# One decoder layer on one NeuronCore: first modulation in groups of 2, 4, 4, 4 and 2 tiles, requested ahead, and six weight slots with extra ones later

## The chip, the cores and the metric

One core of a Trainium2 chip runs the whole program. TensorE (PE) multiplies, VectorE (DVE), ScalarE (ACT) and GpSimd (POOL) do the rest, and SyncE (SP) issues the large transfers from HBM. The metric is the device time of the core in microseconds (us).

## What is computed

One layer with `T = 256` tokens and `D = 2048` channels, all in float32. `c_act` is `silu(c)`; the six parts of the modulation are columns of one matrix-vector product.

```python
mod = (c_act @ w_ada[l] + b_ada[l])[:, None, :]
sh1, sc1, gt1, sh2, sc2, gt2 = jnp.split(mod, N_MOD, axis=-1)
h = rms_norm(x, g_mix_norm[l]) * (1.0 + sc1) + sh1
proj = h @ w_in[l]            # differential attention and gated linear attention (GLA) follow
mix = jnp.concatenate([od, og], axis=-1) @ w_o[l]
x = x + gt1 * mix
h2 = rms_norm(x, g_ffn_norm[l]) * (1.0 + sc2) + sh2
u, g = jnp.split(h2 @ w_up[l], 2, axis=-1)
act = jax.nn.gelu(causal_dwconv(g, w_conv[l], b_conv[l]), approximate=False) * u
x = x + gt2 * (act @ w_down[l])
return rms_norm(x, g_final)
```

## The kernel before

**Units.** All large weights come in units of 512 KB. A unit of `w_in`, `w_o`, `w_up` or `w_down` (two tiles of 128 rows by 512 columns) is loaded by `load_unit` (L107) into one of five `raw` slots, split by ACT into its rounded half `wh` (L110) and by DVE into the rest `wl` (L111), and used by 24 matmuls of 256 columns (`b_block`, L129) or 12 of 512 columns (`a_block`, L163): every product is the sum of three. A unit of `w_ada` goes into the same five slots (`raw_a`, L228 or L231); DVE multiplies it by the column of `c_act` and adds it to `acc` (L241, the first one by ACT, L239), and once all of a group are in, PE sums `acc` over its rows (`ps_mod`, L221), and three short DVE instructions (L253 to L256) make shift and scale. There are 192 units of `w_ada` and 392 of the others.

**Stages.** The first projection takes the 16 tiles of the normalised input `hT` in four rounds (`KGROUPS` 2, 4, 4, 6), here called g0 to g3, and in each round nine column blocks of `w_in` (9, 18, 18 and 27 units). Round g needs shift and scale of its own tiles, so `need` drains their part of the modulation. In before this part is cut into eight groups of two tiles (`ADA1`), each eight units of `w_ada` made of two DMAs of 256 KB. The remaining three blocks of `w_in` (24 units, `LATER`) and the output projection `w_o` (32 units, four column blocks) run beside GLA and attention. Then `rsqrt_m2` (L190 to L194) and `norm_T` (L272 to L282) make `h2T`, and the up projection begins with seven column chunks over tiles 0 to 3 and then over tiles 4 to 7 (56 units), whose sums wait in `spill` tiles; the rest of up (120 units) and down (88 units) follow.

**Order.** The units of `w_ada` are made by generators in the list `bg`, in the order first modulation (64 units), gate 1 (32), second modulation `ada2` (4 times 16), gate 2 (32). Each `load_unit` adds `rate` to a credit and lets one step of `bg` run for each whole one; `drain` runs a group to its end at once. The rates are 1.2 in g0 to g2, 1.0 in g3, 0.3 in `LATER` and `w_o`, 1.05 in the first 56 units of up, 0.25 after. The second modulation's first group is drained after `w_o`. From this program a scheduler makes the order on each engine, by a simulated timeline, unless an instruction is pinned by `keep_in_program_order`; the memory of a slot is given out in the program's order.

**Low rank and tables.** After the second block of every half round, two matmuls for each tile (`ps_low`, L687) add to the low-rank gate input `lowT`. `setup_consts`, run in g0, loads `wlow` (64-byte rows) and the attention tables on ACT's queue and makes the tables on POOL and DVE.

Of the kernel before, what the change touches and what calls it, by code (L numbers as in the profile page):

```python
# [15 lines left out]
P = 128  # L16
# [16 lines left out]
R_K, R_LAST, R_LATER, R_WO, R_SP, R_UP = 1.2, 1.0, 0.3, 0.3, 1.05, 0.25  # L33
# [4 lines left out]
ADA1 = (2, 2, 2, 2, 2, 2, 2, 2)  # L38
# [8 lines left out]
def tile_decoder_layer(  # L47
# [13 lines left out]
    RAW, WH, WL = 5, 3, 3  # L61
# [13 lines left out]
    fg, fcredit, frate = [], [0.0], [0.0]  # L75

# [19 lines left out]

    def load_unit(view, kt, c0):
# [8 lines left out]
        raw = stage.tile([P, 2, 512], F32, tag="raw", name="raw", bufs=RAW)  # L106
        nc.sync.dma_start(out=raw, in_=view[:, kt:kt + 2, c0:c0 + 512])  # L107
        h = stage.tile([P, 2, 512], F32R, tag="wh", name="wh", bufs=WH)
        l = stage.tile([P, 2, 512], F32R, tag="wl", name="wl", bufs=WL)
# [97 lines left out]
    def ada_gen(segs, width, c0, finish, psp, on_pe=(), by_rows=False):  # L207
# [6 lines left out]
        n_end = sum(k in on_pe for k in (KT - 2, KT - 1)) // 2 * 2  # L214
# [9 lines left out]
        for kt in range(0, KT, per):  # L224
            raw = stage.tile([P, per, n], F32, tag="raw", name="raw_a", bufs=RAW)
            rv = raw.rearrange("p k (s n) -> p k s n", n=width)
            if per == 1:
                nc.sync.dma_start(out=rv[:, 0], in_=w_ada4[:, kt, segs[0]:segs[-1] + 1, c0:c0 + width])  # L228
            else:
                for i, sg in enumerate(segs):  # L230
                    nc.sync.dma_start(  # L231
                        out=rv[:, :, i], in_=w_ada4[:, kt:kt + per, sg, c0:c0 + width])
            for j in range(per):
# [13 lines left out]
        finish(acc if by_rows else ps)  # L247
# [47 lines left out]
    colst = t1.tile([3 * KT, P], F32, tag="w4", name="colst", bufs=3)  # L295
    bst = t1.tile([6 * KT, P], F32, tag="w4", name="bst", bufs=3)
# [33 lines left out]

    def setup_consts():
        dlam = t1.tile([P, 6, 64], F32, tag="w4", name="dlam", bufs=3)
        dl2 = dlam[:, 4:6]
        wlow = t1.tile([P, KT, 16], F32, tag="w4", name="wlow", bufs=3)
        cz = t1.tile([P, NTB, T], F32, tag="w4", name="cz", bufs=3)
        nc.scalar.dma_start(out=wlow, in_=w_in_v[:, :, C_LOW:C_LOW + 16])
        nc.scalar.dma_start(out=gdiff, in_=g_diff_subln[0].partition_broadcast(P))
        nc.scalar.dma_start(out=ggla, in_=g_gla_norm[0].partition_broadcast(P))
        nc.scalar.dma_start(out=dlam[:, 0:4], in_=diff_lambda[0].partition_broadcast(P))
        A.activation(wlow2[:, :, 0:16], wlow, AF.Copy)  # L340
        V.tensor_tensor(wlow2[:, :, 16:32], wlow, wlow2[:, :, 0:16], op=ALU.subtract)
# [7 lines left out]
        V.tensor_scalar(neglam, neglam, -LAM_INIT, None, op0=ALU.add)  # L349

# [5 lines left out]
        V.tensor_copy(causal, cz)  # L356
# [3 lines left out]
        for l in range(NLEV + 2):  # L360
            cf = t1.tile([P, P], F32, tag="w4", name="cf", bufs=3)
# [20 lines left out]
            V.tensor_copy(cmat[:, l], cf)  # L382

        for l in range(NLEV):
            h = 1 << l
            nb = P // (2 * h)
            mf = t1.tile([P, P], F32, tag="w4", name="mf", bufs=3)
# [7 lines left out]
            V.tensor_copy(masks[:, l], mf)  # L395
# [229 lines left out]
    ada1 = {}  # L625
    for g, n in enumerate(ADA1):
# [49 lines left out]
    def in_block(bi, ps, kts, first, last):  # L676
# [3 lines left out]
        if bi != 1:  # L680
            return
# [301 lines left out]
```

## Time and profile before

| | us |
|---|---|
| median of three runs (1321.17, 1325.51, 1321.63) | 1321.63 |
| the profiled execution, its own time | 1323.78 |
| its span | 1322.1 |
| PE busy | 1247.1 |
| DVE busy | 898.2 |
| ACT busy | 701.4 |

The program moves 314.59 MB. A profile's "busy" counts an instruction from start to modelled end, so a full PE line can still hide short waits. The granted clock of TensorE is at one of two levels, 1.0 (2.4 GHz) or 0.5 (1.2 GHz); a number between is a mean over the stretch. The DMA share is the mean busy share of the 16 DMA engines.

### The profile page before, as it was taken

How to read it: one execution, taken by the hardware profiler on the slowest of the kernel's cores; microseconds unless marked ns; L12 is line 12 of the kernel's file. 1: busy time of each engine (PE TensorE's matmuls, PEld its weight loads, DVE VectorE, ACT ScalarE, POOL GpSimd, SP SyncE). 2: the span in 40 equal slices, each digit the busy share in tenths (PEclk: the TensorE clock that was granted, in tenths of full speed). 3: DMA queues.
4: the chain of work that ended last, by engine and by line, in shares of the span. 5: the costliest groups of instructions: out<-in, count | busy, mean ns of one | idle time of the engine just before them, and what ended most of it. 6: DMA issues, size and time to landing. Idle time of an engine off the chain costs nothing.

```text
span 1322.1 us, 21489 instructions
## 1 busy us (share of the span) xinstructions
PE 1247.1 (94%) x8492; PEld 1147.9 (87%) x8492; DVE 898.2 (68%) x1198; ACT 701.4 (53%) x914; POOL 30.4 (2%) x79
## 2 busy tenths in 40 slices
PE   4869889999999998799999999999999999999996
PEld 4658778899888998799999999999999988888885
DVE  4787787987666677768776687776666554545454
ACT  4546666674554543455767566654444443434343
POOL 1700000000000000000000000000000000000000
PEclk8879999999998999899999999999999999999998
DMA  8899999976466467889998777677777755555562
GB/s 273 272 300 299 300 301 315 305 254 204 144 190 206 145 209 254 283 293 315 318 332 278 232 230 234 208 220 232 224 229 232 243 188 191 194 194 195 181 205 98
DMA packets 172884, 314.59 MB, mean 238 GB/s; under 512 B 12813, under 2 KB 46285, under 8 KB 172782
## 3 DMA queue, kind: packets, MB, share of 16 engines
q1 hardware_dynamic: 168384, 307.28, 72.8%
q10 hardware_dynamic: 4398, 5.93, 1.3%
q8 instruction: 66, 1.08, 0.3%
q14 instruction: 36, 0.29, 0.1%
HBM read 311.07 MB, written 2.10 MB: 237 GB/s over the span
## 4 chain that ended last, share of the span: by engine, by line
PE 63%; DMA 20%; DVE 9%; issue 3%; ACT 2%; POOL 2%; SPq 0%; DVEq 0%; ACTq 0%; POOLq 0%
PE ps_h L129 27%; PE ps_d L163 18%; DMA raw_a<-in_w_ada_dram 14%; PE ps_o L129 5%; PE ps_mm L129 4%; DMA raw<-in_w_in_dram 4%; DVE acc L241 4%; DVE wl L111 3%; PE ps_mm L163 3%; DMA raw<-in_w_up_dram 2%; ACT wh L110 2%; PE ps_s L558 1%; DMA xtok<-in_x_dram 1%; PE ps_a L501 1%; PE ps_s L556 0%
## 5 line engine op out<-in xcount | busy, mean ns | idle before, releaser
L110 ACT ACTIVATE wh<-raw 128x1024 fp32r<-128x1024 f32 x392 | 414.3, 1058 | 462.7 <-PE ps_h L129 138.0
L111 DVE TENSOR_TENSOR wl<-raw,wh 128x1024 fp32r<-128x1024 f32 x392 | 478.5, 1223 | 253.5 <-ACT wh L110 250.6
L129 PE MATMUL ps_h<-h2T,wh 128*128 128x256 f32 x2816 | 511.2, 284 | 7.9 <-ACT h2T L277 6.7
L129 PEld LDWEIGHTS ps_h<-h2T,wh 128*128 128x128 f32 x2816 | 441.0, 193 | 8.9 <-ACT h2T L277 7.1
L129 PE MATMUL ps_h<-h2T,wl 128*128 128x256 f32 x1408 | 400.4, 285 | 4.8 <-DVE wl L111 4.7
L241 DVE SCALAR_TENSOR_TENSOR acc<-raw_a,cols,acc 128x512 f32<-128x512 f32 (+1 forms) x237 | 240.8, 1018 | 110.7 <-DMA raw_a<-in_w_ada_dram 106.2
L129 PEld LDWEIGHTS ps_h<-h2T,wl 128*128 128x128 f32 x1408 | 271.0, 193 | 6.8 <-DVE wl L111 6.7
L163 PE MATMUL ps_d<-wh,act 128*128 128x512 f32 x704 | 217.4, 389 | 0.8 <-DVE dx L941 0.8
L163 PEld LDWEIGHTS ps_d<-wh,act 128*128 128x128 f32 x704 | 132.2, 188 | 29.2 <-DVE dx L941 1.2
L129 PE MATMUL ps_mm<-hT,wh 128*128 128x256 f32 x768 | 146.9, 291 | 10.2 <-ACT hT L281 3.7
L163 PE MATMUL ps_d<-wl,act 128*128 128x512 f32 x352 | 137.8, 391 | 0.0
L129 PEld LDWEIGHTS ps_mm<-hT,wh 128*128 128x128 f32 x768 | 123.6, 197 | 13.8 <-ACT wh L110 4.1
L163 PE MATMUL ps_mm<-wh,hT 128*128 128x512 f32 x384 | 122.8, 394 | 2.8 <-ACT pj_gq L731 1.1
L129 PE MATMUL ps_mm<-hT,wl 128*128 128x256 f32 x384 | 111.9, 292 | 4.7 <-DVE wl L111 4.6
L129 PE MATMUL ps_o<-mixT,wh 128*128 128x256 f32 x512 | 97.6, 292 | 2.3 <-DVE xT L783 2.3
L163 PEld LDWEIGHTS ps_mm<-wh,hT 128*128 128x128 f32 x384 | 72.2, 188 | 19.8 <-ACT wh L110 1.8
L129 PEld LDWEIGHTS ps_o<-mixT,wh 128*128 128x128 f32 x512 | 82.7, 198 | 4.2 <-DVE xT L783 2.7
L163 PE MATMUL ps_mm<-wl,hT 128*128 128x512 f32 x192 | 77.2, 402 | 6.8 <-DVE wl L111 6.7
L129 PEld LDWEIGHTS ps_mm<-hT,wl 128*128 128x128 f32 x384 | 75.3, 196 | 6.5 <-DVE wl L111 6.1
L163 PEld LDWEIGHTS ps_d<-wl,act 128*128 128x128 f32 x352 | 66.1, 188 | 13.9 <-issue 0.5
L129 PE MATMUL ps_o<-mixT,wl 128*128 128x256 f32 x256 | 75.1, 293 | 1.5 <-DVE wl L111 1.5
L129 PEld LDWEIGHTS ps_o<-mixT,wl 128*128 128x128 f32 x256 | 50.8, 198 | 2.9 <-DVE wl L111 2.2
(237 smaller groups left out, 864.6 us busy)
## 6 DMA issues: line engine op xcount, KB each, us to landing
raw<-in_w_up_dram SPq DMA_DIRECT2D x176, 512.0 KB, 4.6
raw_a<-in_w_ada_dram SPq DMA_DIRECT2D x128, 512.0 KB, 5.0
raw<-in_w_in_dram SPq DMA_DIRECT2D x96, 512.0 KB, 5.5
raw<-in_w_down_dram SPq DMA_DIRECT2D x88, 512.0 KB, 4.5
raw_a<-in_w_ada_dram SPq DMA_DIRECT2D x128, 256.0 KB, 4.7
raw<-in_w_o_dram SPq DMA_DIRECT2D x32, 512.0 KB, 4.4
xtok<-in_x_dram ACTq DMA_DIRECT2D x4, 512.0 KB, 10.1
gfin<-in_g_final_dram ACTq DMA_DIRECT2D x2, 512.0 KB
```

The source lines that it names most:

```text
L110: A.activation(h, raw, AF.Copy)
L111: V.tensor_tensor(l, raw, h, op=ALU.subtract)
L129: PE.matmul(ps[:, m * T:(m + 1) * T], w[:, j, ms], xt[k][:, xx, :], start=(first and k == kts[0] and m % 2 == 0 and i == 0), stop=(last an ...
L163: PE.matmul(ps[:, tb * 512:(tb + 1) * 512], xt[k][:, xx, tsl], w[:, j, :], start=(first and k == kts[0] and i == 0), stop=(last and k == k ...
L241: V.scalar_tensor_tensor(acc, raw[:, j], col, acc, op0=ALU.mult, op1=ALU.add)
L501: PE.matmul(pv[:, i, tb], lhs, rhs, start=True, stop=True)
L558: PE.matmul(pv, q[rs, hb * T + tb * P:hb * T + (tb + 1) * P], k[rs, hb * T:hb * T + n], start=False, stop=(tb == 1), skip_group_check=True)
```

## The change

- The first modulation is cut into groups of 2, 4, 4, 4 and 2 tiles. A group of four is 16 units, each one DMA of 512 KB and one DVE instruction of 1024 columns. Its groups and the making of `hT` (`norm_gen`) stand in `bg` one behind the other, and the rates are 2.2, 1.15, 1.3 and 1.0 in the four rounds, and the steps that run in one round are those of the next round's modulation.
- In the first two groups of the list (`early`) a unit is requested one step before it is used, and its DVE or ACT instructions are pinned.
- The tables are made in g1, one step for each `load_unit`; `wlow` is loaded in g2; the low-rank product is made at once, in g3.
- Six `raw` slots in place of five; room for it comes from smaller temporary tiles (tag `w2`). From the first spill round to chunk 7 of up, two more `raw` slots, one `wh` and one `wl` lie in the memory of the last two chunks' `act` tiles (`late`, `slot`).
- Rates of 0.5 in `LATER`, 0.8 in `w_o`, 0.9 in the first part of up, 0.27 after; `ada2_0` is drained before the last block of `w_o`, where the rate is then 0. The ends of the modulation, `rsqrt_m2` and `norm_T` have high priority with the scheduler.

```diff
-R_K, R_LAST, R_LATER, R_WO, R_SP, R_UP = 1.2, 1.0, 0.3, 0.3, 1.05, 0.25
+R_K, R_LATER, R_WO, R_SP, R_UP = (2.2, 1.15, 1.3, 1.0), 0.5, 0.8, 0.9, 0.27
-ADA1 = (2, 2, 2, 2, 2, 2, 2, 2)
+ADA1 = ((2,), (4,), (4,), (4, 2))
-    RAW, WH, WL = 5, 3, 3
+    RAW, WH, WL = 6, 3, 3
+    spare, turn = {}, {"raw": 0, "wh": 0, "wl": 0}
+    def slot(tag, shape, dtype, name, bufs):
+        extra = spare.get(tag, [])
+        turn[tag] = turn[tag] % (bufs + len(extra)) + 1
+        if turn[tag] > bufs:
+            return extra[turn[tag] - bufs - 1].rearrange("p (a b) -> p a b", a=shape[1])
+        return stage.tile(shape, dtype, tag=tag, name=name, bufs=bufs)
...
-        raw = stage.tile([P, 2, 512], F32, tag="raw", name="raw", bufs=RAW)
+        if setup and next(setup[0], "end") == "end":
+            setup.pop(0)
+        raw = slot("raw", [P, 2, 512], F32, "raw", RAW)
...
-        for kt in range(0, KT, per):
-            raw = stage.tile([P, per, n], F32, tag="raw", name="raw_a", bufs=RAW)
+        def load(kt):
+            raw = slot("raw", [P, per, n], F32, "raw_a", RAW)
...
+        pin = tc.keep_in_program_order if early else lambda ins: ins
+        if early:
+            ahead = load(0)
+            yield
+        for kt in range(0, KT, per):
+            if early:
+                raw, ahead = ahead, load(kt + per) if kt + per < KT else None
+            else:
+                raw = load(kt)
...
-                    V.scalar_tensor_tensor(acc, raw[:, j], col, acc, op0=ALU.mult, op1=ALU.add)
+                    pin(V.scalar_tensor_tensor(acc, raw[:, j], col, acc, op0=ALU.mult, op1=ALU.add))
...
+    def norm_gen(kts):
+        for k in kts[::2]:
+            with tc.high_priority():
+                hT.extend(norm_T(t1, rst1, s1, sh1, k, f"hT{k}", 1 if k == 0 else 2))
+            yield
+    for g, kts in enumerate(KG):
+        k0 = kts[0]
+        for n in ADA1[g]:
+            bg.append(("ada1", ada_gen((0, 1), n * P, k0 * P, mod_cols(s1, sh1, 0, GM, k0, n), get_ps,
+                                       FIRST_PE if g == 0 else (), early=g < 2)))
+            bg.append((f"norm{k0}", norm_gen(list(range(k0, k0 + n)))))
+            k0 += n
...
+    def low_gates():
+        pl = pss.tile([P, 512], F32, tag="ms", name="ps_low")
+        for k in range(KT):
             for xx in range(2):
                 PE.matmul(pl[0:32, 0:T], wlow2[:, k, :], hT[k][:, xx, :],
...
+        drain(f"norm{kts[0]}")
+        rate[0] = R_K[g]
+        if g == 1:
+            setup.append(setup_consts())
...
     for nb in range(2, 4):
+        if nb == 3:
+            drain("ada2_0")
+            rate[0] = 0.0
         wo_part(nb, psm.tile([P, 1024], F32, tag="mm", name="ps_o"), 0, KT)
-    rate[0] = 0.0
-    drain("ada2_0")
...
+    late = [actp.tile([P, 2, 1024], t, tag=f"act{ch}", name=f"late{ch}") for ch, t in ((NCH - 2, F32), (NCH - 1, F32R))]
+    spare.update(raw=[late[0][:, i] for i in range(2)], wh=[late[1][:, 0]], wl=[late[1][:, 1]])
...
+        if ch == NCH - 4:
+            spare.clear()
```

Three places show how the order moves. First SP's queue in round g0, before (`raw` is a unit of `w_in`, `raw_a` one of `w_ada`, the two DMAs of a unit merged as x2):

```order
L231 DMA raw_a_304<-in_w_ada_dram 128x2x256 x2
L107 DMA raw_309<-in_w_in_dram 128x2x512
L231 DMA raw_a_340<-in_w_ada_dram 128x2x256 x2
L107 DMA raw_345<-in_w_in_dram 128x2x512
L231 DMA raw_a_516<-in_w_ada_dram 128x2x256 x2
L107 DMA raw_521<-in_w_in_dram 128x2x512
```

SP's queue at the same place after:

```order
L240 DMA raw_a_302<-in_w_ada_dram 128x2x512
L240 DMA raw_a_305<-in_w_ada_dram 128x2x512
L120 DMA raw_308<-in_w_in_dram 128x2x512
L240 DMA raw_a_339<-in_w_ada_dram 128x2x512
L240 DMA raw_a_342<-in_w_ada_dram 128x2x512
L120 DMA raw_345<-in_w_in_dram 128x2x512
```

Two units of `w_ada`, of the next round's group, now stand before most units of `w_in` in g0. Second, DVE's queue between `w_o` and up, before (`rst` and `rt` are the normalisation's factors, `xv` and `h2T` the new input):

```order
L241 SCALAR_TENSOR_TENSOR acc<-raw_a,cols,acc 128x1024
L192 TENSOR_TENSOR rt_5357<-rst_184 128x256
L111 TENSOR_TENSOR wl<-raw,wh 128x1024
L193 SCALAR_TENSOR_TENSOR rt_5357<-ps_q,rt_5357 128x256
L241 SCALAR_TENSOR_TENSOR acc<-raw_a,cols,acc 128x1024
L194 SCALAR_TENSOR_TENSOR rst_184<-rt_5357,rst_184 128x256
L272 TENSOR_TENSOR xv<-xT,rst_184 128x256 x2
```

DVE's queue at the same place after:

```order
L820 SCALAR_TENSOR_TENSOR xT<-ps_o,gt_87,xT 128x256 x2
L124 TENSOR_TENSOR wl<-raw,wh 128x1024
L205 TENSOR_TENSOR rt_5244<-rst_188 128x256
L206 SCALAR_TENSOR_TENSOR rt_5244<-ps_q,rt_5244 128x256
L207 SCALAR_TENSOR_TENSOR rst_188<-rt_5244,rst_188 128x256
L297 TENSOR_TENSOR xv<-xT,rst_188 128x256
```

One `wl` and two `acc` have left the chain from `ps_q` to `h2T`. Third, PE's queue at one of the low-rank products, before:

```order
L163 MATMUL ps_mm<-wh,hT_844 128x512
L687 MATMUL ps_low<-hT_1430,wlow_130 32x256 x4
L129 MATMUL ps_mm<-hT_1347,wh 128x256 x2
L129 MATMUL ps_mm<-hT_1347,wl 128x256
L129 MATMUL ps_mm<-hT_1347,wh 128x256 x2
```

PE's queue in round g3 after, where the last half of them stands:

```order
L142 MATMUL ps_mm<-hT_1889,wl 128x256
L719 MATMUL ps_low<-hT_1120,wlow_130 32x256 x4
L719 MATMUL ps_low<-hT_1576,wlow_130 32x256 x4
L719 MATMUL ps_low<-hT_1583,wlow_130 32x256 x4
L719 MATMUL ps_low<-hT_1889,wlow_130 32x256 x4
L176 MATMUL ps_mm<-wh,hT_1576 128x512
```

All 32 now stand in g3, in two clusters of 16. Counted over SP's whole queue, the units requested up to the last weight of each stage are, before and after: g0 27 and 33, g1 69 and 70, g2 106 and 108, g3 159 and 159, `LATER` 191 and 194, third block of `w_o` 224 and 237, fourth 234 and 245, the two spill rounds 349 and 345.

## Rows read from the trace of the kernel before

**Rows 1.** Busy time by stretch: us, engines (instructions), granted clock, DMA share, GB/s.

```profile
core 0: us, PE busy (x) PEld busy (x) DVE busy (x) ACT busy (x) POOL busy (x), PEclk, DMA share, GB/s
10.00:20.00 10.00, 5.04 (x22) 4.46 (x22) 5.14 (x15) 7.04 (x15) 0.00 (x0) 1.00 0.98 340
...
60.00:80.00 20.00, 16.52 (x116) 14.66 (x115) 15.15 (x23) 11.36 (x13) 0.00 (x0) 1.00 0.92 292
80.00:100.00 20.00, 11.32 (x62) 10.55 (x62) 16.18 (x25) 8.81 (x11) 0.00 (x0) 0.66 0.99 310
100.00:150.00 50.00, 48.42 (x289) 42.36 (x289) 40.81 (x57) 34.44 (x39) 0.00 (x0) 1.00 0.94 302
...
200.00:240.00 40.00, 37.16 (x233) 31.72 (x231) 31.28 (x36) 26.80 (x32) 0.00 (x0) 1.00 0.96 325
240.00:310.00 70.00, 68.77 (x426) 61.86 (x427) 62.35 (x112) 45.60 (x63) 0.00 (x0) 1.00 0.85 272
...
410.00:505.00 95.00, 94.75 (x709) 87.81 (x710) 62.33 (x119) 45.55 (x102) 0.00 (x0) 0.96 0.56 182
505.00:548.00 43.00, 31.54 (x213) 29.63 (x212) 36.30 (x50) 15.36 (x24) 0.00 (x0) 0.84 0.86 290
548.00:720.00 172.00, 166.98 (x1375) 164.70 (x1375) 124.72 (x117) 110.88 (x123) 0.00 (x0) 1.00 0.90 305
720.00:1068.00 348.00, 348.00 (x2902) 347.91 (x2901) 236.98 (x255) 186.99 (x207) 0.00 (x0) 1.00 0.74 228
```

**Rows 2.** Waits of SP's issuing queue, 0 to 240 us: total, times, longest.

```profile
SPq L231 <- DVE wl L111: 41.5, 27, 3.5
SPq L231 <- DVE acc L241: 19.2, 17, 5.2
```

**Rows 3.** Waits of SP's issuing queue, 548 to 720 us.

```profile
SPq L107 <- DVE wl L111: 31.6, 25, 2.5
SPq L107 <- DVE acc L241: 27.5, 26, 1.4
```

**Rows 4.** As Rows 1 without POOL, instructions on `acc` alone, first 60 us.

```profile
0.00:60.00 60.00, 2.42 (x14) 2.52 (x14) 20.65 (x28) 2.15 (x3) 0.86 0.88 268
```

**Rows 5.** Waits of PE, 60 to 240 us, the two longest.

```profile
PE ps_mod L221 <- DVE acc L241: 4.2, 1, 4.2
PE ps_mm L129 <- ACT hT L281: 3.7, 1, 3.7
```

**Rows 6.** Groups of instructions, shapes apart: count, busy us, mean ns, idle before.

```profile
L241 DVE SCALAR_TENSOR_TENSOR acc<-raw_a,cols,acc 128x1024 f32<-128x1024 f32 x120 | 153.8, 1282 | 88.0 <-DMA raw_a<-in_w_ada_dram 88.0
L241 DVE SCALAR_TENSOR_TENSOR acc<-raw_a,cols,acc 128x512 f32<-128x512 f32 x117 | 87.0, 748 | 22.6 <-DMA raw_a<-in_w_ada_dram 18.2 <-ACT acc L239 3.2
L687 PE MATMUL ps_low<-hT,wlow 128*32 128x256 f32 x32 | 6.0, 297 | 1.7 <-ACT hT L277 1.7
```

**Rows 7.** The chain that ended last: start us, length us, what.

```profile
929.38 138.23 PE ps_h L129 x1152
```

**Rows 8.** Order of time between `w_o` and up: start us, us, engine, instruction, [idle before].

```profile
525.13 0.50 PE L129 MATMUL ps_o<-mixT,wh 128*128 128x256 f32 x2 [2.03 <-DVE xT L783]
...
532.04 1.11 PE L795 MATMUL ps_q<-sq,ones 128*128 128x256 f32 x4
...
535.26 0.42 DVE L192 TENSOR_TENSOR rt<-rst 128x256 f32<-128x256 f32 x1
...
535.60 1.22 DVE L111 TENSOR_TENSOR wl<-raw,wh 128x1024 fp32r<-128x1024 f32 x1
536.73 0.42 DVE L193 SCALAR_TENSOR_TENSOR rt<-ps_q,rt 128x256 f32<-128x256 f32 x1
...
537.07 1.28 DVE L241 SCALAR_TENSOR_TENSOR acc<-raw_a,cols,acc 128x1024 f32<-128x1024 f32 x1
538.26 0.42 DVE L194 SCALAR_TENSOR_TENSOR rst<-rt,rst 128x256 f32<-128x256 f32 x1
...
539.83 0.80 PE L129 MATMUL ps_h<-h2T,wh 128*128 128x256 f32 x2 [6.68 <-ACT h2T L277]
```

More of the change, by code (lines that the diff above doesn't have):

```diff
@@ L238, in ada_gen @@
                 elif kt + j == 0:
-                    A.activation(acc, raw[:, j], AF.Copy, scale=col)
+                    pin(A.activation(acc, raw[:, j], AF.Copy, scale=col))
                 else:
-                    V.scalar_tensor_tensor(acc, raw[:, j], col, acc, op0=ALU.mult, op1=ALU.add)
-            if not by_rows and (kt + per == KT - n_end or kt + per == KT and not n_end):
+                    pin(V.scalar_tensor_tensor(acc, raw[:, j], col, acc, op0=ALU.mult, op1=ALU.add))
+            if not by_rows and kt + per == KT:
                 if not on_pe:
@@ L624, in tile_decoder_layer @@
     KG = [list(range(sum(KGROUPS[:g]), sum(KGROUPS[:g + 1]))) for g in range(len(KGROUPS))]
[L625 to L630 removed]
+    hT = []
+    def norm_gen(kts):
+        for k in kts[::2]:
+            with tc.high_priority():
+                hT.extend(norm_T(t1, rst1, s1, sh1, k, f"hT{k}", 1 if k == 0 else 2))
+            yield
+    for g, kts in enumerate(KG):
[5 more added lines that the diff above has]
+            k0 += n
     for hf in range(2):
@@ L717, in tile_decoder_layer @@
         A.activation(xT[:, k:k + 2], ps.rearrange("p (a b) -> p a b", b=T), AF.Copy)
-    need([1])
     for g, kts in enumerate(KG):
         last = g == len(KG) - 1
-        rate[0] = R_LAST if last else R_K
+        drain(f"norm{kts[0]}")
+        rate[0] = R_K[g]
+        if g == 1:
+            setup.append(setup_consts())
+        if g == len(KG) - 2:
+            tc.keep_in_program_order(nc.scalar.dma_start(out=wlow, in_=w_in_v[:, :, C_LOW:C_LOW + 16]))
+        if last:
+            setup_low()
         def open_block(bi):
@@ L747, in tile_decoder_layer @@
                 in_block(bi, lead[bi], ks, g == 0 and i == 0, i == len(halves) - 1)
+                if last and bi == 1 and i == len(halves) - 1:
+                    low_gates()
                 if i == len(halves) - 1:
@@ L827, in need2 @@
             drain(f"ada2_{k // 4}")
-            h2T.extend(norm_T(tmp, rst2, s2, sh2, k, f"h2T{k}", 1 if k == 0 else 2))
+            with tc.high_priority():
+                h2T.extend(norm_T(tmp, rst2, s2, sh2, k, f"h2T{k}", 1 if k == 0 else 2))
     UG = [list(range(sum(UGROUPS[:g]), sum(UGROUPS[:g + 1]))) for g in range(len(UGROUPS))]
```

92 lines of the change are left out of this document (41 added, 51 removed).

## The prediction

> **What bounds the kernel now.** I read the busy times by stretch first [rows 1]. From 720 us on PE is busy all the time (348.00 of 348), and the long piece of the chain says at which pace: 1152 matmuls in 138.23 us, 0.120 us each [rows 7]. So the second half of up, and down behind it, can give nothing to a change that only moves loads and DVE work. PE stands idle at four places before that. From 60 to 240 us it is busy 16.52 of 20, 11.32 of 20, 48.42 of 50 and 37.16 of 40 us, while the DMA engines are busy 0.92 to 0.99 and move 292 to 325 GB/s [rows 1]: here the transfers pace the program. From 505 to 548 us it is busy 31.54 of 43 us, at a mean clock of 0.84 [rows 1]. From 548 to 720 us it is busy 166.98 of 172, again at a DMA share of 0.90 [rows 1]. Between these, in attention and the output projection, PE is full (94.75 of 95 us from 410 us on) and the transfers are not: 0.56 of the engines' time, 182 GB/s [rows 1]. The modulation's bytes are thus loaded where transfers are short, and hardly where they are free.
>
> Second view: what SP's queue waits for. From 0 to 240 us its DMAs wait 41.5 us for `wl` and 19.2 us for `acc`, from 548 to 720 us 31.6 and 27.5 us [rows 2, 3]: DVE has to empty a slot before SP may ask for the next unit. Five slots leave the engines 4 to 10 per cent idle in stretches that they pace. Third view: PE's own waits there are 4.2 us for the sum of one modulation group and 3.7 us for the `hT` behind it [rows 5], a group that came after its weights.
>
> **The change part by part.** The profiled execution took 1323.78 us; its sum is made against that, and the median of the three runs is 2.15 us below it.
>
> *First projection, 0 to 310 us.* The number of units up to the end of g3 is the same, 159, and within two at the ends of g1 and g2, so nothing is saved but time per unit. A unit is 0.524 MB; at 302 GB/s [rows 1] it takes 1.74 us. Six slots in place of five let one more unit be on its way; DVE empties the slots faster too, since 48 units of two 748 ns instructions become 48 of one 1282 ns instruction [rows 6], 48 x 0.214 = 10.3 us less of the work on which SP waits. Ends for the new rate: 310 GB/s, the rate of 80 to 100 us at a share of 0.99, and 340 GB/s, that of 10 to 20 us at 0.98 [rows 1]. I take 320 (1.64 us), between the 310 and the 325 of 200 to 240 us, the rows of the same mixture of units. From the 27th unit (near 60 us) to the 131st, in the middle of g3, after which PE is full (68.77 of 70 us [rows 1]), that is 104 x 0.10 = 10 us; with the ends 5 and 20. In the first 60 us the share is 0.88 [rows 4]; with the tables and `wlow` out of the way and one more slot I put it at 0.93, 60 x (1 - 0.88/0.93) = 3 us, between 0 and 5. Sum -13. That g0 now carries six more units delays its weights, not the end of g3: those units are missing later. The 4.2 and 3.7 us of PE go, since each group is done a round ahead, but they are not added: PE would then wait for transfers instead.
>
> The table work of POOL and DVE moves from g0 to g1; DVE has 9.2 us free in each 50 there (40.81 busy [rows 1]), and no table is needed before attention, so 0. The low-rank product costs 32 matmuls of 256 columns [rows 6] at 0.120 us, 3.8 us, which lay in the idle stretches; in g3 they stand in two clusters of 16 where PE is idle between 7 per cent (200 to 240 us) and 2 per cent [rows 1]. Between 0 and +4: +2.
>
> *Attention and output projection, 310 to 505 us.* Before the fourth block of `w_o`, 13 more units of the modulation are requested (237 against 224). Transfers have room. DVE gets 13 x 1.282 = 17 us more; from 410 to 505 us it is busy 62.33 of 95 us [rows 1]. An `acc` that waits for its data holds up the `wl` behind it on DVE's queue, and PE waits for that. Against it, gate 1 is complete before its drain, and the clock's 0.96 from 410 us on [rows 1], 7.6 us at half speed, may go. From -4 to +8; I take 0, as PE hides nearly all of DVE there now.
>
> *Between the two projections, 505 to 548 us.* PE is idle 11.5 us, and 0.84 means 13.8 us at half clock [rows 1]. In the chain from `ps_q` (ends at 533.15) to the first `ps_h` (539.83), three short DVE instructions stand 1.5 us apart because a `wl` of 1.22 and an `acc` of 1.28 us lie between them, and the first waits for an `acc` ahead [rows 8]. After, the order has them back to back: 2.2 us and about 1 us gone. Ahead of `ps_q`, PE's waits are mostly behind the drained `acc` (2.03 us for `xT` alone [rows 8]): 11.5 - 6.7 - 1 for the first tile = 3.8 us, gone with the drain, since the fourth block has no modulation in it. Of the half clock, 2 us. Sum -9, from -3 (the chain alone) to -14.
>
> *First part of up, 548 to 720 us.* From the first weight on, 115 units become 100. At 305 GB/s [rows 1] a unit takes 1.72 us: 198 us of transfers against 56 x 24 x 0.120 = 161 us of PE before, and after, with the six that the slots already hold, 94 x 1.72 = 162 us, even without the two extra slots, which are to raise the share of 0.90. PE's idle 5.0 us here plus the waits too short for the view: -6, from 0 to -8. The first request into the extra slots waits for DVE's first `h2T`, and SP's queue behind it; 12 units stand before it and only six slots, so SP does not come there before PE starts: at most 2 us, inside the ends. The rest, from 720 us: `y` has two buffers in place of three, but each is needed again only two chunks (16 units of 2.9 us at the least) later: 0.
>
> Sum: -13 + 2 + 0 - 9 - 6 = -26 us; 1323.8 - 26 = 1297.8, and 2.15 less for the median: **1296 us**.
>
> A row on sizes: the modulation's 256 KB DMAs moved 340 GB/s (10 to 20 us), the mixture with 512 KB 302 [rows 1], so a larger DMA buys nothing that this trace shows. The Trainium skill, "DMA: Bandwidth & Descriptors", section "Rules for kernel authors", asks for 1 MiB and more per DMA for full bandwidth; by it the joined DMAs would carry more. With the 358 GB/s that the same page gives as HBM's limit for a core, my estimate by that page for the 104 units would be 28 us in place of 10, and the time 1278 us; no row here reaches that rate.
>
> **The rivals.**
>
> *The engines are full already.* A share of 0.94 to 0.99 speaks for it, 340 GB/s at 0.98 against it [rows 1]. The first projection then gives 0: -13, 1309 us.
>
> *The queue reaches its best row.* At 340 GB/s in the first projection, 20 + 5 - 2 in place of 13 - 2: -38, 1284 us. Less DVE work speaks for it; the 310 at a share of 0.99 against. The page's rule on the size of DMAs points this way too, and past it.
>
> *The moved modulation lands on the path.* All of the 17 us of DVE hold up attention or `w_o`: -26 + 17 = -9, 1313 us; together with full engines +4, no difference that can be measured. DVE's 33 us free of 95 speak against.
>
> *Slower: PE at half clock through g1.* In g0 two or three units now come for each unit of weights, (33/9) x 1.64 = 6.0 us for 2.9 us of matmuls. From 80 to 100 us the trace shows what waiting does: PE idle 8.7 of 20 us, clock 0.66, that is 13.6 us at 1.2 GHz [rows 1]. At half clock a unit takes 5.8 us; in g0 that hides behind the transfers, in g1 (37 units for 18 weights, 3.4 us each) it does not: 18 x 2.4 = 43 us if it stays so for the whole round, against -26: +17, 1339 us. It decides if the clock is still 0.5 when more than about 11 of the 18 units of g1 are done. Against it: once PE had work in a row, from 100 us on, the clock was 1.00 [rows 1], and a PE at half clock with weights waiting is never idle. The Trainium skill, "TensorE: Matmul & The Clock Gate", section "HAM oscillation — how this bites in real kernels", says that bursts of matmuls shorter than the wait for the next slice bring the clock down each time; by that rule the rival is the likely course in g0. The row of 80 to 100 us agrees, that of 60 to 80 us, with PE idle 3.5 of 20 us and a clock of 1.00, does not.
>
> **How the numbers follow.** The forecast, 1286 to 1307 us, 0.56; best row, 0.10; full engines, 0.13; moved modulation, 0.09, of which 0.05 with full engines (no difference); half clock, 0.06; something not seen, 0.06, spread over all. About 0.3 per cent, 4 us, is what a measurement can tell from no change. Faster: 0.56 + 0.10 + 0.13 + 0.04 + 0.05 = 0.88; the same 0.06; slower 0.06. The range takes in the best row and the full engines and ends at the moved modulation: 1279 to 1313 us; some 0.06 lies below and 0.13 above.
>
> **What would show it.** In the first projection: a DMA share of 0.97 and more from 60 us to the end of g2, 315 to 325 GB/s, SP's waits for `wl` and `acc` below 40 us in sum, the last unit of g2 landing some 12 us earlier; PE's waits for `ps_mod` and `hT` gone. From `ps_q` to `ps_h` about 3.5 us instead of 6.7. In the first part of up, PE idle under 2 us at a lower rate than 305 GB/s. Wrong is the forecast if the share rises and the rate does not, if PE's line between `w_o`'s first and third block gets gaps behind `wl`, or if the granted clock in g1 is 0.5.

## The result, and the profile after

The changed kernel takes 1301.8 us (median, 1299.9 to 1305.5) against 1321.4 us of the kernel before: ratio 0.9849, 95% interval 0.9819 to 0.9879, 19.6 us less. The forecast was 1296 us. The two profiled executions took 1301.91 and 1323.78 us, 21.9 us apart. This table has where each stage ends on PE (start of its last matmul, us), and how far the changed kernel is ahead of the one before:

```
stage ends                      before    after   ahead   forecast for the step
g2, third quarter of first proj.  209.1    187.0    22.0
g3, first projection              311.1    291.8    19.4   13, less 2 for low rank
attention's own projections       407.0    390.5    16.5   )
first two w_o blocks              477.2    472.3     4.9   ) 0
third w_o block                   500.4    495.4     5.0   )
fourth w_o block                  529.1    519.9     9.2   } 9
first matmul of up                539.8    526.6    13.2   }
first half of up's first part     631.3    612.6    18.7   ) 6
second half                       720.4    696.8    23.6   )
up                               1067.3   1045.8    21.6   0
```

Busy time of the changed kernel by stretch, columns as in [rows 1]:

```profile
60.00:80.00 20.00, 17.38 (x110) 15.63 (x109) 15.99 (x20) 15.51 (x20) 0.85 (x2) 0.91 1.00 348
80.00:100.00 20.00, 19.27 (x119) 17.12 (x118) 18.25 (x22) 12.55 (x13) 14.00 (x26) 1.00 1.01 346
100.00:150.00 50.00, 48.29 (x307) 43.01 (x306) 41.97 (x48) 35.47 (x39) 13.37 (x27) 1.00 1.00 340
200.00:240.00 40.00, 40.00 (x216) 33.74 (x215) 33.70 (x45) 26.30 (x35) 0.00 (x0) 1.00 0.95 314
...
410.00:505.00 95.00, 87.86 (x644) 81.56 (x643) 62.41 (x116) 42.39 (x94) 0.00 (x0) 0.93 0.61 189
505.00:548.00 43.00, 35.62 (x268) 34.22 (x268) 30.41 (x37) 20.13 (x28) 0.00 (x0) 0.92 0.71 233
548.00:720.00 172.00, 172.00 (x1439) 172.00 (x1438) 124.89 (x122) 114.38 (x126) 0.00 (x0) 1.00 0.90 310
```

From 60 to 150 us the rate is 340 to 348 GB/s where [rows 1] has 292 to 310, and PE is nearly full. From 548 us on PE is busy all of 172 us (166.98 before). But from 410 to 505 us, where PE was full for 94.75 us, it is busy 87.86 at a lower clock, and by the table the first two `w_o` blocks gave 11.6 us back (16.5 us ahead, then 4.9). On SP's queue, 0 to 240 us, [rows 2] has two of the six lines on `wl` and `acc` of the kernel before. The other four are these:

```profile
SPq L107 <- DVE acc L241: 18.6, 21, 2.5
SPq L107 <- DVE wl L111: 15.9, 14, 2.4
SPq L228 <- DVE wl L111: 10.3, 6, 2.4
SPq L228 <- DVE acc L241: 3.7, 3, 1.4
```

The changed kernel has (L240 and L243 are the modulation's loads, L120 the weights'):

```profile
SPq L240 <- DVE wl L124: 37.2, 28, 2.8
SPq L120 <- DVE wl L124: 29.3, 23, 2.4
SPq L240 <- DVE acc L265: 24.8, 24, 2.4
SPq L120 <- DVE acc L265: 24.6, 30, 1.4
SPq L243 <- DVE acc L265: 5.9, 4, 2.7
```

With 1.7 us more at L243 for `wl` these are 123.5 us, against 109.2 before. The waits grew a little and the DMA engines are full all the same, at a share of 1.00 from 60 to 150 us: the sum of SP's waits does not tell what the transfers lose. From `ps_q` to up's first matmul, in order of time (start, us, engine, instruction), to be laid beside [rows 8]:

```profile
522.00 1.13 PE L832 MATMUL ps_q<-sq,ones 128*128 128x256 f32 x4 [1.37 <-ACT sq L826]
...
524.13 0.42 DVE L205 TENSOR_TENSOR rt<-rst 128x256 f32<-128x256 f32 x1 [1.16 <-ACT rst L204]
524.58 0.42 DVE L206 SCALAR_TENSOR_TENSOR rt<-ps_q,rt 128x256 f32<-128x256 f32 x1
525.04 0.42 DVE L207 SCALAR_TENSOR_TENSOR rst<-rt,rst 128x256 f32<-128x256 f32 x1
...
526.61 0.58 PE L142 MATMUL ps_h<-h2T,wh 128*128 128x256 f32 x1 [3.48 <-ACT h2T L302]
```

The three short instructions stand 0.45 us apart, not 1.5, and PE waits 3.48 us, not 6.68. And this is PE's order near the end of the first two `w_o` blocks, where the gain went back (`cst` are four small tables of the convolution, the fourth is its bias; `ps_cv` is made from them):

```profile
455.53 0.26 PE L850 MATMUL ps_cv<-ident,cst 44*128 44x44 f32 x1 [0.34 <-ACT nconv L851]
459.26 0.30 PE L850 MATMUL ps_cv<-ident,cst 44*128 44x44 f32 x1 [3.48 <-DMA cst<-in_b_conv_dram]
459.50 3.57 PE L233 MATMUL ps_mod<-ones,acc 128*128 128x1 f32 x16
462.93 0.67 PE L648 MATMUL ps_ot<-ident,pj_dq 128*128 128x128 f32 x2
464.29 1.31 PE L142 MATMUL ps_o<-mixT,wh 128*128 128x256 f32 x3 [0.69 <-ACT mixT L475]
```

Three questions followed: what lifted the rate, what gave 11.6 us back, and what filled up's first part.

### The profile page after: what moved, and what is told of

It is laid out like the page before. It is cut to its first block, busy times and chain, and to the rows that moved or that the text cites. A ratio compares the mean times of both kernels' runs of the same rounds, so it can differ in the third digit from the quotient of the medians.

```text
span 1300.2 us, 21317 instructions
## 1 busy us (share of the span) xinstructions
PE 1239.3 (95%) x8492; PEld 1145.4 (88%) x8492; DVE 888.1 (68%) x1137; ACT 702.3 (54%) x913; POOL 38.3 (3%) x79
## 4 chain that ended last, share of the span: by engine, by line
PE 82%; DMA 8%; DVE 5%; ACT 2%; issue 2%; DVEq 0%; ACTq 0%
PE ps_h L142 39%; PE ps_d L176 18%; PE ps_mm L142 8%; PE ps_mm L176 6%; DMA raw_a<-in_w_ada_dram 5%; PE ps_o L142 5%; DVE acc L265 2%; DMA raw<-in_w_in_dram 2%; DVE wl L124 1%; PE ps_mod L233 1%; PE ps_s L590 1%; ACT wh L123 1%; PE ps_a L533 1%; DMA xtok<-in_x_dram 1%; DMA dlam<-in_diff_lambda_dram 1%
## 5 line engine op out<-in xcount | busy, mean ns | idle before, releaser
L124 DVE TENSOR_TENSOR wl<-raw,wh 128x1024 fp32r<-128x1024 f32 x339 | 413.9, 1223 | 220.2 <-ACT wh L123 218.9
L123 ACT ACTIVATE wh<-raw 128x1024 fp32r<-128x1024 f32 x339 | 357.6, 1057 | 372.1 <-PE ps_d L176 123.0
L142 PE MATMUL ps_h<-h2T,wh 128*128 128x256 f32 x2304 | 419.2, 284 | 4.7 <-ACT h2T L302 3.5
L142 PEld LDWEIGHTS ps_h<-h2T,wh 128*128 128x128 f32 x2304 | 360.7, 193 | 5.4 <-ACT h2T L302 3.9
L142 PE MATMUL ps_h<-h2T,wl 128*128 128x256 f32 x1152 | 326.7, 284 | 0.0
L265 DVE SCALAR_TENSOR_TENSOR acc<-raw_a,cols,acc 128x1024 f32<-128x1024 f32 (+1 forms) x180 | 216.3, 1202 | 89.5 <-DMA raw_a<-in_w_ada_dram 88.0
L142 PEld LDWEIGHTS ps_h<-h2T,wl 128*128 128x128 f32 x1152 | 221.7, 192 | 0.0
L142 PE MATMUL ps_h<-h2T,late 128*128 128x256 f32 x768 | 97.4, 283 | 0.0
L142 PEld LDWEIGHTS ps_h<-h2T,late 128*128 128x128 f32 x768 | 94.4, 192 | 0.0
```

The costliest lines, as they stand in the source:

```text
L123: A.activation(h, raw, AF.Copy)
L124: V.tensor_tensor(l, raw, h, op=ALU.subtract)
L142: PE.matmul(ps[:, m * T:(m + 1) * T], w[:, j, ms], xt[k][:, xx, :], start=(first and k == kts[0] and m % 2 == 0 and i == 0), stop=(last an ...
L265: pin(V.scalar_tensor_tensor(acc, raw[:, j], col, acc, op0=ALU.mult, op1=ALU.add))
```

## What lifted the rate of the first projection

**Five slots.** The slot alone undone:

```diff
-    RAW, WH, WL = 6, 3, 3
+    RAW, WH, WL = 5, 3, 3
```

> The changed kernel with five weight slots instead of six (one number); the groups of 2, 4, 4, 4, 2 tiles, the early requests and the moved tables stay. Theory A (the sixth slot gave the first projection's 340 to 348 GB/s, since one more 512 KB request is always queued): between 60 and 200 us the rate falls back to 302 to 325 GB/s, end of the third quarter of the first projection 10 to 20 us later than the changed kernel's 187.0 us, total 1311 to 1321 us. Rival B (the rate came from rows of 2 KB in place of 1 KB and from fewer, longer sums on DVE, not from the slot): the rate stays above 335 GB/s and the total within 4 us of 1301.8.

Measured: 1328.3 us, ratio to the kernel before 1.0057 (1.0031 to 1.0082), slower than before the change. g2 ends at 206.5 us, 19.4 later than with six; another 8 us are lost by the end of attention's projections. Theory A held, and by more than it said.

**Short rows.** Each 512 KB modulation load as two of 256 KB, in 1 KB rows:

```diff
-                nc.sync.dma_start(out=rv[:, 0], in_=w_ada4[:, kt, segs[0]:segs[-1] + 1, c0:c0 + width])
+                for o in ((0, width // 2) if segs == (0, 1) else (None,)):
+                    w2 = slice(0, width) if o is None else slice(o, o + width // 2)
+                    nc.sync.dma_start(out=rv[:, 0, :, w2], in_=w_ada4[:, kt, segs[0]:segs[-1] + 1, c0 + w2.start:c0 + w2.stop])
```

> The changed kernel in which each 512 KB request of the first modulation's groups of four tiles is issued as two of 256 KB with rows of 1 KB, as the kernel before has them; slots, sums and order stay. Rival B of the run with five slots, in its form 'row length': the rate between 60 and 200 us falls from 340-348 to 300-325 GB/s and the total is 8 to 15 us longer (1310 to 1317). Theory A (the sixth slot): rate above 335 GB/s, total within 3 us of 1301.8.

Measured: 1303.8 us, 0.9859 (0.9835 to 0.9882), g2 at 187.4 us. Size and row length of these loads make no difference here that can be measured.

**The kernel before with six slots.** Its edit is `RAW` 5 to 6, with the small tables on the smaller buffer `w2`, `sq` in a projection tile and two `y` buffers:

```diff
-    RAW, WH, WL = 5, 3, 3
+    RAW, WH, WL = 6, 3, 3
...
-        y = t2.tile([P, 4, T], F32, tag="w4", name="y", bufs=3)
+        y = t2.tile([P, 4, T], F32, tag="w4", name="y", bufs=2)
```

> The kernel before with six weight slots and what makes room for them (small tables in a smaller buffer, the square of x in a projection tile, two y buffers); groups of two tiles, early tables and the old rates of filler work stay. Theory A (the slot alone gives the rate): the first projection goes at 335 to 348 GB/s from 60 us on and ends 12 to 20 us earlier; total 1301 to 1310. Rival B (the slot helps only with the regrouped modulation): the rate stays at 302 to 320 GB/s, total 1316 to 1324.

Measured: 1314.2 us, 0.9936 (0.9915 to 0.9958). g2 ends at 196.2 us (12.9 ahead of before), g3 at 292.7 (18.4 ahead). Theory A's 18 us came and nearly its rate (332 GB/s), its total did not: 7.9 us went back in the first half of up's first part (99.4 us against 91.5). PE waits there 5.4 us at once for a `wl` that stands on DVE behind a sum for whose transfer DVE waits 4.7 us.

**Small groups.** The changed kernel with groups of two tiles:

```diff
-ADA1 = ((2,), (4,), (4,), (4, 2))
+ADA1 = ((2,), (2, 2), (2, 2), (2, 2, 2))
```

> The changed kernel with the first modulation again in groups of two tiles (2 in place of each 4), everything else kept: six slots, early requests, moved tables, spare late slots. Theory (the sixth slot carries the first projection's gain, the grouping only DVE time that is not on the path): rate between 60 and 200 us stays above 330 GB/s, end of the third quarter within 5 us of 187.0, total within 4 us of 1301.8. Rival (longer rows and half as many short sums are what lets the slot be used, since the kernel before with six slots and small groups ended its third quarter 9 us later): third quarter ends 6 to 12 us later, total 1307 to 1313.

Measured: 1310.6 us, 0.9919 (0.9892 to 0.9947), g2 at 195.7 us. The rival held: grouping is worth 9 us on top of the slot. The transfers of the five kernels from 60 to 200 us, one line each (packets, bytes, mean rate, small packets): the changed one, five slots, short rows, before with six slots, small groups.

```profile
DMA packets 28593, 48.18 MB, mean 344 GB/s; under 512 B 3697, under 2 KB 7921, under 8 KB 28579
```

```profile
DMA packets 26943, 43.76 MB, mean 313 GB/s; under 512 B 3569, under 2 KB 7770, under 8 KB 26931
```

```profile
DMA packets 37195, 47.97 MB, mean 343 GB/s; under 512 B 4206, under 2 KB 24814, under 8 KB 37182
```

```profile
DMA packets 36546, 46.48 MB, mean 332 GB/s; under 512 B 2187, under 2 KB 25883, under 8 KB 36535
```

```profile
DMA packets 36609, 44.70 MB, mean 319 GB/s; under 512 B 4130, under 2 KB 25631, under 8 KB 36597
```

The third line has three times the packets under 2 KB of the first, and its rate. Ahead at the end of g2: slot alone 12.9 us, everything but the slot 2.6, everything but the grouping 13.4, all 22.0. The two parts are not a sum; the slot pays in full only with the groups of four. Why they do is open: not the loads (short rows); the sums are candidates, since from 60 to 200 us DVE spends 82 x 748 ns on 41 units with small groups, 1.50 us a unit against 1.28 [rows 6], and so is the place where a group's sum falls due. Against the sums' work as the only cause: from 150 to 200 us both kernels with small groups move 343 GB/s, with sums of the same small size, and the changed one 347; the small-group run is behind at 60 to 80, 80 to 100 and 100 to 150 us, with 274, 315 and 315 GB/s. Early requests and moved tables show nothing of their own by that time: small groups with them (195.7) and without (196.2) end g2 together.

## What gave 11.6 us back in the output projection

**Fourth table.** A buffer of its own for the table that PE waited 3.48 us for:

```diff
-        cst = t1.tile([FT, P], F32, tag="w2", name="cst", bufs=3)
+        cst = t1.tile([FT, P], F32, tag="w2" if j < 3 else "cst3", name="cst", bufs=3 if j < 3 else 1)
```

> The changed kernel with a buffer of its own for the fourth table of the second projection's gates (the one whose transfer PE waits 3.5 us for at 455 us, with the engine in order behind it). Theory: that wait and the half clock which follows it cost 5 to 9 us of the path; total 1293 to 1297, last w_o block ends 5 to 9 us earlier than 519.9. Rival: the next wait in the row (the gate's sums for mixT, which end at 460.9 us on DVE) takes its place; the PE wait is renamed, total within 2 us of 1301.8.

Measured: 1303.8 us, 0.9853 (0.9834 to 0.9872). The wait is gone and the first two blocks still take 78.9 us (81.8 changed, 70.2 before); PE waits for `mixT` instead. The rival held.

**First product on DVE.** So that ACT does not hold `mixT` behind a transfer, first alone, then together with the fourth table's own buffer:

```diff
-                    pin(A.activation(acc, raw[:, j], AF.Copy, scale=col))
+                    pin(A.activation(acc, raw[:, j], AF.Copy, scale=col)) if segs == (0, 1) else V.tensor_scalar(acc, raw[:, j], col, None, op0=ALU.mult)
```

> The changed kernel with the first product of each later modulation sum on DVE in place of ACT, so that ACT no longer waits 2.7 us for a modulation transfer at 442 us while it holds the copy of mixT that PE needs. Theory: the 2 us PE wait and the half clock after it go, 3 to 6 us; total 1296 to 1299. Rival: DVE waits in its place and holds the second half of mixT, or the next transfer does; total within 2 us of 1301.8.

> Both removals at once: the fourth table in its own buffer and the first product of the later sums on DVE. Theory (the two PE waits of the first two w_o blocks are one after the other, each refilled by the other or by the half clock, and only the removal of both shows): the two blocks take 72 to 76 us, total 1292 to 1297. Rival (the blocks are bound by the chains of the gate and of attention, at 461 us, whatever PE waits for first): they take 78 to 82 us, total within 3 us of 1301.8.

Measured: 1300.1 us, 0.9841 (0.9809 to 0.9873), and with both edits 1301.4 us, 0.9848 (0.9817 to 0.9879); the blocks take 80.2 and 78.4 us. PE's longest waits are then for `pj_dq` (1.8) and `mixT` (1.8): each wait taken away was renamed. Both rivals held.

**Old rates.** Filler modulation after the first projection at the old rates, so that the program puts 4 steps and not 13 among the units of the first two blocks:

```diff
-R_K, R_LATER, R_WO, R_SP, R_UP = (2.2, 1.15, 1.3, 1.0), 0.5, 0.8, 0.9, 0.27
+R_K, R_LATER, R_WO, R_SP, R_UP = (2.2, 1.15, 1.3, 1.0), 0.3, 0.3, 1.05, 0.25
```

> The changed kernel with the old rates of filler modulation after the first projection (0.3, 0.3, 1.05, 0.25 in place of 0.5, 0.8, 0.9, 0.27), so that less modulation stands in attention and w_o and more in the spilled chunks. Theory C (the modulation moved into the first two w_o blocks gives back some 11 us: 81.8 us for them against 70.2): these blocks take 70 to 74 us, and the whole gains 5 to 10 us (1292 to 1297), if the first part of the up-projection still hides what comes back to it. Rival (the w_o blocks lose because attention's chains, which are no faster, are reached sooner): they take 79 to 83 us, total within 4 us of 1301.8 or above.

Measured: 1298.9 us, 0.9821 (0.9793 to 0.9850). The two blocks take 70.3 us, as theory C said; 5.3 us of it go back in the third block, where most of the group's steps are drained, and 1.7 in the fourth. The total is 2.9 us less than the changed kernel's, short of the 5 to 10 that the theory had, and the two intervals overlap.

**Spread.** As few steps in the first two blocks, the rest in the third and fourth:

```diff
-R_K, R_LATER, R_WO, R_SP, R_UP = (2.2, 1.15, 1.3, 1.0), 0.5, 0.8, 0.9, 0.27
+R_K, R_LATER, R_WO, R_SP, R_UP = (2.2, 1.15, 1.3, 1.0), 0.3, 0.25, 1.05, 0.25
...
-        if nb == 3:
-            drain("ada2_0")
-            rate[0] = 0.0
+        rate[0] = 0.9
...
+    drain("ada2_0")
```

> The changed kernel with the filler modulation spread otherwise: old rate in attention, 4 steps (not 13) in the first two w_o blocks, 7 in the third and 7 in the fourth, and the old rate in the spilled chunks. Theory C (a step costs about 1.2 us where attention's chains run and nothing in the third and fourth block): first two w_o blocks 69 to 73 us (81.8 changed, 70.2 before), third 23 to 24, fourth 24 to 27, total 1288 to 1294. Rival (the second group of the later modulation then comes too late for the fourth block or the up-projection, as the drain of 10 steps ahead of the fourth block cost 5 us): fourth block or the stretch to the first product of the up-projection 5 or more us longer, total 1296 to 1300.

**Third block.** The old rates, with one line more:

```diff
+        if nb == 2:
+            rate[0] = 1.0
```

> The run with the old rates of filler work, with one more line: in the third w_o block the rate is 1.0 in place of 0.3, so that 8 of the 10 outstanding steps of the second modulation's first group stand among that block's units and 2 or 3, not 7, are drained behind it. Theory (the drained steps made the third block 28.4 us against 23.1, by PE's wait for the last sum and the half clock behind it): third block 23 to 25 us, first two blocks 70 to 72 us at full clock as with the old rates, total 1293 to 1297. Rival (the order that the scheduler finds decides more than the number of steps: the spread run had as few steps in the first two blocks and lost 9 us there at half clock): the first two blocks take 79 us or more again with a granted clock below 0.95 in their second half, total 1300 to 1309.

Measured: 1308.7 us, 0.9897 (0.9862 to 0.9933), and 1301.9 us, 0.9829 (0.9801 to 0.9856). The first two blocks take 79.6 and 80.1 us. The spread run lies outside both of its forecasts, and its fourth block takes 30.2 us against 24.6. The third-block run came out as its rival said. The second halves of the two blocks, busy time as in [rows 1], the changed kernel first, then old rates, then the third-block run:

```profile
426.50:472.30 45.80, 38.66 (x259) 35.29 (x257) 27.07 (x62) 19.75 (x54) 0.00 (x0) 0.85 0.54 171
```

```profile
427.20:458.70 31.50, 28.88 (x226) 27.02 (x225) 20.51 (x42) 14.72 (x37) 0.00 (x0) 1.00 0.56 176
```

```profile
427.90:467.70 39.80, 30.80 (x225) 28.71 (x224) 25.52 (x46) 15.63 (x38) 0.00 (x0) 0.91 0.58 187
```

But the two runs did not keep the steps out of these blocks. SP requests the third block's units from 435 to 438 us on, while PE is still in the second half of the first two, and the steps that the program puts among those units run then too. In the first and the second half DVE and ACT start 8 and 6 sums of the modulation (`acc`) in the changed kernel, 3 and 2 before, 3 and 3 with old rates, but 2 and 7 in the spread run and 3 and 7 in the third-block run. Instructions on `acc` alone in the second half (columns as in [rows 4]), old rates, then the third-block run:

```profile
427.20:458.70 31.50, 0.00 (x0) 0.00 (x0) 3.85 (x3) 0.00 (x0) 1.00 0.56 176
```

```profile
427.90:467.70 39.80, 0.00 (x0) 0.00 (x0) 8.99 (x7) 0.00 (x0) 0.91 0.58 187
```

Of all fourteen kernels three keep the clock at 1.00 through this half, before, before with six slots and old rates. They have 2 or 3 sums there, DVE stands idle 1.8 to 4.7 us for the sums' transfers, and the half takes 28.6 to 31.5 us. The other eleven have 6 or 7 sums and 5.3 to 10.9 us of such idle time, fall to 0.85 to 0.93 and take 38.7 to 46.3. So the two runs do not speak against theory C: the sums that they meant to keep out ran there all the same. In the first half no such split shows: 8 sums go with 35.1 to 44.1 us there, 2 or 3 with 38.8 to 41.6. At 0.85 some 30 per cent of the 45.8 us, 13.7, were at 1.2 GHz; by estimate at most half of that, 6.9 us, is lost to the clock, and waits are the rest.

How a sum costs time shows on DVE's queue. Old rates, then the third-block run, in order of time on DVE:

```profile
447.13 0.15 DVE L205 TENSOR_TENSOR ods<-ods 128x2 f32<-128x2 f32 x1
447.20 1.22 DVE L124 TENSOR_TENSOR wl<-raw,wh 128x1024 fp32r<-128x1024 f32 x1
448.34 0.15 DVE L206 SCALAR_TENSOR_TENSOR ods<-ods,ods 128x2 f32<-128x2 f32 x1
448.53 0.16 DVE L207 SCALAR_TENSOR_TENSOR ods<-ods,ods 128x2 f32<-128x2 f32 x1
448.72 0.16 DVE L635 TENSOR_TENSOR ods<-ods,st 128x2 f32<-128x2 f32 x1
448.92 0.61 DVE L637 SCALAR_TENSOR_TENSOR pj_dq<-ps_od,ods,gdiff 128x128 f32<-128x128 f32 x2
```

```profile
448.27 0.15 DVE L205 TENSOR_TENSOR ods<-ods 128x2 f32<-128x2 f32 x1
...
449.67 0.16 DVE L207 SCALAR_TENSOR_TENSOR ods<-ods,ods 128x2 f32<-128x2 f32 x1
451.30 1.29 DVE L265 SCALAR_TENSOR_TENSOR acc<-raw_a,cols,acc 128x1024 f32<-128x1024 f32 x1 [1.47 <-DMA raw_a<-in_w_ada_dram]
452.50 0.15 DVE L635 TENSOR_TENSOR ods<-ods,st 128x2 f32<-128x2 f32 x1
452.57 1.22 DVE L124 TENSOR_TENSOR wl<-raw,wh 128x1024 fp32r<-128x1024 f32 x1
453.71 0.60 DVE L637 SCALAR_TENSOR_TENSOR pj_dq<-ps_od,ods,gdiff 128x128 f32<-128x128 f32 x2
455.43 1.28 DVE L265 SCALAR_TENSOR_TENSOR acc<-raw_a,cols,acc 128x1024 f32<-128x1024 f32 x1 [1.12 <-DMA raw_a<-in_w_ada_dram]
456.63 0.68 DVE L476 TENSOR_TENSOR mixT<-ps_ot,mixT 128x512 fp32r<-128x512 f32 x1
```

The lines from L205 to L637 are one chain, the normalisation of differential attention's output, and PE waits for its end, `pj_dq`. From L205 to `pj_dq` it is 1.8 us in the one and 5.4 us in the other: there a sum that waits 1.47 us for its transfer stands inside the chain, another one ahead of `mixT`, and what is behind them on DVE waits with them. PE's line in the third-block run at that place, where old rates have a wait of 0.16 us for `pj_dq`:

```profile
451.59 0.23 PE L850 MATMUL ps_cv<-ident,cst 44*128 44x44 f32 x1 [1.94 <-DMA cst<-in_b_conv_dram]
454.11 0.73 PE L648 MATMUL ps_ot<-ident,pj_dq 128*128 128x128 f32 x2 [2.29 <-DVE pj_dq L637]
```

PE is busy 0.96 of the 5 us from 450 on in that run, and the granted clock is 0.50 in the 5 us behind them. PE's order is the same in these two kernels through those blocks. In the changed kernel it is ACT that holds a `mixT`, behind a first product that waits 2.73 us for its transfer, and PE waits 1.95 us for it. In the spread run a sum that waits 2.94 us stands ahead of an `xT`, and PE waits 4.37 us for that. So in these three kernels sums that wait for their transfers hold PE up. That the new rates cost the 11.6 us is shown by the old rates; how much of it is such holding up is not shown, nor whether the number of sums in the second half counts or their place in the order: no kernel here has many of them there and is fast.

## What filled up's first part

**No spare slots**, and **only the two weight slots** of them:

```diff
-    spare.update(raw=[late[0][:, i] for i in range(2)], wh=[late[1][:, 0]], wl=[late[1][:, 1]])
```

```diff
-    spare.update(raw=[late[0][:, i] for i in range(2)], wh=[late[1][:, 0]], wl=[late[1][:, 1]])
+    spare.update(raw=[late[0][:, i] for i in range(2)])
```

> The changed kernel without the spare slots in the act tiles of the last chunks (two more weight slots, one more for each half of a split), so that the first part of the up-projection goes with six slots. Theory: the 10.4 us that the first part gained (85.9 and 84.2 us for its halves against 91.5 and 89.1) came from the spare slots; without them the halves take 88 to 92 us and the total is 5 to 10 us longer (1307 to 1312). Rival: they came from the sixth slot and the new order of the modulation; halves within 1 us of 85.9 and 84.2, total within 3 us of 1301.8.

> The changed kernel with only the two spare weight slots in the last chunks' tiles, without the spare halves of a split. Theory (the first part of the up-projection is fed by requests in flight: eight weight slots against six): its halves take 86 and 84 us as in the changed kernel, total within 3 us of 1301.8. Rival (three split pairs bound it: a slot comes free only when DVE has written the low half, which waits for PE to leave the pair): halves 90 to 93 and 88 to 90 us, total 1310 to 1319.

Measured: 1319.4 us, 0.9986 (0.9972 to 1.0001), and 1308.7 us, 0.9901 (0.9876 to 0.9927). Without spares the halves take 93.0 and 90.3 us, with weight slots alone 87.2 and 87.6, with all 86.0 and 84.2. So the spares are worth 13.2 us there, 8.5 by the weight slots and 4.7 by the split halves, and from up's first to its last matmul, where work that only moved drops out, 12.5 us, 5.3 and 7.2 (531.7, 526.4 and 519.2 us); the theory of the first run held, with a larger loss than it said, and neither forecast of the second did. Busy time from 548 to 720 us without spares:

```profile
548.00:720.00 172.00, 165.79 (x1342) 164.48 (x1341) 114.13 (x109) 108.87 (x121) 0.00 (x0) 0.97 0.86 281
```

Rate 281 GB/s against 310. The first of the two runs lost 5.5 us more in the fourth `w_o` block: without the spares two more sums run there on DVE, and one of them, which waits 1.68 us for its transfer, stands ahead of the `xT` that PE waits for. The changed kernel waits 1.3 us for `xT` at most there.

```profile
PE ps_o L142 <- DVE xT L820: 4.6, 1, 4.6
```

No version beat the changed kernel beyond doubt: old rates, 1298.9 us, has an interval that overlaps its own.

## Why the prediction was right, and which steps were not

**Direction and range** held: 1301.8 us lies between 1279 and 1313. Two terms were too small and one should not have been 0: 10.7 us were gained beyond the sum in the first projection and in up, and 14.4 us were lost where 0 stood. In those places two rivals came nearly true, the best row (0.10) and the moved modulation (0.09). That these nearly cancel, and the total lies near 1296, is luck.

**First projection, -13: mis-sized.** By g2 it was -22.0, 19.4 of it by g3. The step that failed is "I take 320 (1.64 us), between the 310 and the 325": the rate was 338 to 344, which the prediction had as a rival with a chance of 0.10. The row of 310 GB/s at a share of 0.99 was held against the higher rate. It is no limit: the changed kernel moves 340 to 348 at 1.00 and 1.01. The cause was named rightly in part: the slot is the larger part, as the five-slot run shows, but not alone. SP's waits for `wl` and `acc`, forecast below 40 us, are 123.5 us: that sign was wrong. It was also misread, since 41.5 and 19.2 us are two lines of six and the six were 109.2 us before (and from 548 to 720 us 31.6 and 27.5 are two of four, 98.7 us in all). Of the size of a load the prediction said that it buys nothing; short rows bear this out. The rule that it was weighed against (the Trainium skill, "DMA: Bandwidth & Descriptors", "Rules for kernel authors") asks for loads of 1 MiB and more; here modulation loads of 256 KB and of 512 KB gave 343 and 344 GB/s, so with six slots the trace shows no gain from 256 to 512 KB; 1 MiB was not tried.

**Low-rank part, +2**: g3 gave back 2.7 us, of which PE's longest wait is 1.8 us for `pj_gg`, a tile of GLA's gate. Its share was not measured alone.

**Attention and output projection, 0: wrong.** It cost 2.8 us in attention and 11.6 us in the first two blocks. The mechanism stood in the text ("an `acc` that waits for its data holds up the `wl` behind it on DVE's queue"), and so did 8 us as its end; it was set to 0 since "PE hides nearly all of DVE there". That step counted DVE's busy time, 17 us, against its idle time. What the traces show is that DVE stands idle for the transfers of the sums in the second half of the two blocks, ahead of what PE needs, and the half clock behind PE's stalls, which the sum priced only as a gain. The rival priced at 17 us came nearly whole, with 14.4 us. The text had gaps behind `wl` as a sign of being wrong: PE got gaps there, of 3.5 us behind `cst` and 2.6 behind `mixT`, and none behind `wl`.

**Between the projections, -9**: 4.2 us in the fourth block and 4.0 us from there to up's first matmul, -8.2. Right, step by step: 3.48 us was forecast as about 3.5.

**First part of up, -6: too small**, -10.4, or -8.3 without work that only moved. The bound of -8 came from PE's idle 5.0 us and waits too short for the view. From up's first matmul to the end of the part PE was idle 6.1 us of 180.6 before and 1.3 of 170.2 after, so 5.6 of the 10.4 us lay inside the time that counts as busy; some 2 of these are work that moved out of the part (the next paragraph). The run without the spare slots took 183.3 us for the part, more than before.

**From 720 us on, 0**: up's last stretch takes 2.0 us more (349.0 against 347.0 us), but this is moved work. Of 32 transposes (`ps_y`), 19 ran before that stretch in the kernel before, and all 32 run in it after; PE waits for nothing there in either. So up as a whole gained 8.3 us (527.5 against 519.2 from its first to its last matmul), and the 0 holds.

**Half clock through g1**: not realised. From 32 to 60 us the clock was 0.78, as the rival said of g0, though hardly lower than the 0.82 before, but from 80 us on it was 1.00, and g1 took 55.8 us (72.1 before). The section that the rival drew on ("HAM oscillation — how this bites in real kernels" in the Trainium skill's "TensorE: Matmul & The Clock Gate") tells of bursts of matmuls shorter than the wait for the next transfer, which bring the clock down each time. Such a course did not come in g1. In `w_o` the trace agrees as far as one wait goes: behind PE's 3.48 us for the fourth table the granted clock was 0.50.

## What to carry to other kernels

Where a stretch is paced by transfers, look at the best rate of the trace before taking a DMA share near 1 for the limit; one more slot may be worth more than all else, and less with small groups of the other work that shares it. Filler work that waits for a transfer must be priced by what stands behind it on its engine's queue, not by its busy time: with 3 sums of it in the second half of the two `w_o` blocks they took 70.3 us, with 7 there 80.1. And look in the trace where such work runs: steps meant for the third block ran in the first two. Take a wait away only after looking at what is late next: three removals of a named wait brought nothing that could be measured.

## What the runs showed of the hardware

Busy time of the changed kernel around the wait for the fourth table stands below, columns as in [rows 1]. First, the DMA share passes 1: short rows had 1.06 at 357 GB/s from 60 to 80 us, so a share of 1.00 does not mean that nothing more can be had. And a short stall is dear: in the changed kernel PE ran no matmul from 455.8 to 459.2 us, and over the next 5.1 us the granted clock was 0.50; the 16 matmuls of `ps_mod` took 3.57 us there, and the same 16 took 1.84 us before (from 530.34 us on).

```profile
455.80:459.20 3.40, 0.00 (x0) 0.00 (x0) 1.28 (x6) 0.77 (x5) 0.00 (x0) 0.76 0.84 280
459.20:464.30 5.10, 4.35 (x20) 3.90 (x20) 2.08 (x7) 0.80 (x2) 0.00 (x0) 0.50 0.44 140
```
